# A gated-convolution and recurrence layer on one core: 1/rms by way of DRAM, one more gate group ahead, other buffers for three low halves, an earlier load of p

## The chip, the cores and the metric

One core of a Trainium2 chip runs the whole kernel in one launch. Its engines are TensorE (PE; matmuls, with the loads of weights, PEld, beside them), VectorE (DVE), ScalarE (ACT), GpSimd (POOL) and SyncE (SP). Here SP issues most loads of weights and POOL issues the other transfers. The metric is the device time of one execution in microseconds, as the median of several runs.

## What is computed

The layer takes 2,048 tokens of a prompt and 64 of a second sequence, 1,024 channels each. Cut to what matters here:

```python
h = rms_norm(x, g_pre)                       # x / rms(x) * g_pre
proj = einsum('btd,dn->btn', h, w_in)        # ten times 1,024 columns
vA, bA, cA, zA, q, f, iv, zB, gA, gB = split_cols(proj)
yA = einsum('btc,cd->btd', silu(zA) * bA * causal_conv3(cA * vA, conv_w), w_a_out)
o  = hgrn2_scan(S0, silu(q), 1 - fg, iv, log(fg))   # fg from f; 8 heads
yB = einsum('btc,cd->btd', rms(o) * g_onorm * silu(zB), w_b_out)
merged = sigmoid(gA) * yA + sigmoid(gB) * yB
x = x + rms_norm(einsum('btd,de->bte', merged, w_o), g_post)
gate = sigmoid(einsum('btd,de->bte', rms_norm(x, g_ple), w_ple_gate))
x = x + einsum('btp,pd->btd', p, w_ple_proj) * gate
```

The results are x of all tokens, the last two rows of the convolution's input and the states of the recurrence. All is float32.

## The kernel before

**Tiles and number form.** The 2,112 tokens are worked on in three blocks of 768, 704 and 640 (`SIZES`). Activations lie with the channels on the partitions: one tile is 128 channels by the tokens of a block, and eight tiles make 1,024 channels. A float32 product is made from two parts of each operand, a high one (rounded) and a low one (the rest), as three matmuls: high by high, high by low, low by high. `split` makes the parts: ScalarE casts the high one (L220, L267) and VectorE subtracts for the low one (L220).

**The seven products.** Most weights are taken in groups of two blocks of 128 columns (`sgroup`, L403). A group is a 2 x 2 scheme with seven products in place of eight. In their order (`PRODUCTS`) these use A11, S3, S1, S2, A12, A22 and S4, where S1 to S4 are sums and differences of A11, A21, A22 and A12. With 4 blocks of channels and 3 matmuls, a product is 12 matmuls and a group 84. L418, L419 and L420 are the three matmuls. Some groups make their sums from raw weights (`combined` with `first`, L335 to L356; the sums at L346); these are block 0's and two of block 1's, the first one and GB6 (the gate group of columns 6 and 7). In these two the low halves of A11, A12 and A22 already lie in DRAM and are loaded. Sums and low halves are stored to DRAM (`keep_sum`, L325; L274) for later blocks, which load them back (`kept_w`).

**The buffers of weights.** The pool `wp` has rotating buffers by tag: `raw` 5, `hi` 4, `lo` 4 and `s` 3. `sum_tile` takes an `s`; `low_tile` (L235) gives a `lo` or, in three of every seven calls, an `s`. A buffer is given again when the last reader of the old tile is done. Activations come from a ring of 48 buffers (`rt`). Matmuls write to five banks of one PSUM pool and three of another.

**The order of a block.** For each block: `path_b` (recurrence heads, with the rest of the gate groups between them), `path_a` (convolution), then the merge with W_A and W_B, the product with W_O, the two norms, and the final gate with W_G. In block 0 the merge is `merge`, with plain matmuls (L600 to L602). In blocks 1 and 2 it is `merge_in_turn`; there and in W_O the seven products of four groups take turns (`in_turn`, L533, matmuls L565 to L567, evictions L588, L590 and L459). The gates of the next block begin before the end of the present one: `run(fills, LEAD)` at L1529 runs seven of its eight gate groups, so that TensorE has work while the norms of W_O's result (`final_norm`, L1267) are made. Their steps are hung between products with `spread_out`, by a list that says how many steps each hook takes.

**1/rms of the next block.** While `path_a` runs, `row_rstd` (L713 to L732) loads x with the tokens on the partitions (L723), squares it with a sum (L729) and gets 1/rms as columns: 128 tokens each, six per block, three for each half. After the merge, `next_ops` (L1492) calls `spread_all` (L671), which for each half makes a matmul per column with the identity (`spread`, L663, matmul L668) to have the values on all partitions, and copies them from PSUM (L675). `operands` then loads x by channels (`load_x`, L710), scales it (`scaled_x`, L752) and splits it. `next_ops` is called in block 0 at step j == 6 of W_B, in block 1 at product 6 of W_B.

**p.** `load_p` (L1129) loads two tiles of p; for the last block it is called at product 5 of W_B, from POOL's queue. The other transfers of this stage there are reloads of gates and outputs (`reload`, L1175).

What sets the order on each engine is a scheduler that goes by priorities: `tc.high_priority`, `issue_after`, and dependencies. All buffers are given in the order of the program's text.

Of the kernel before, what the change touches and what calls it, by code (L numbers as in the profile page):

```python
# [18 lines left out]
P = 128  # L19
# [22 lines left out]

SWAP = 2

LEAD = 7


def plan():
# [45 lines left out]
def hybrid_step(  # L94
# [140 lines left out]
    def low_tile():  # L235

        turn[0] += 1
        if turn[0] % 7 in (1, 3, 5):
            return sum_tile(F32R)
        return wp.tile([P, 4, P], F32R, tag="lo", name=nm("lo"))  # L240
# [13 lines left out]
            return part == 1 and (idx - W_A) % KB >= KH  # L254
        return True

    def split_w(raw, key=None, spread=False):


        hi = wp.tile([P, 4, P], F32R, tag="hi", name=nm("hi"))  # L260
        if spread:
            lo = low_tile()
            split(raw, hi, lo)
            return hi, lo
        if key in lows:
            lo = low_tile()
            A.copy(hi, raw)  # L267
            SP.dma_start(lo.bitcast(F32), lows[key])
            return hi, lo
        lo = wp.tile([P, 4, P], F32R, tag="lo", name=nm("lo"))  # L270
        split(raw, hi, lo)
        if key is not None and used_later(*key):
            lows[key] = dram.tile([P, 4, P], F32, tag=f"lo{key}", name=nm("low"), bufs=1)
            stores[0].dma_start(lows[key], lo.bitcast(F32))  # L274
        return hi, lo
# [59 lines left out]
    def combined(i1, i2, first, anew):  # L335


        with tc.high_priority():
            if not first:
                return {n: kept_w(i1, i2, n, spread=anew) for _, n, _, _, _ in PRODUCTS}  # L340
            a11, a21, a22, a12 = (load_raw(w_blk[i, h]) for i, h in ((i1, 0), (i2, 0), (i2, 1), (i1, 1)))
            out = dict(A11=split_w(a11, (i1, 0)))

            def total(name, x, y, op):
                s = sum_tile()
                V.tensor_tensor(s, x, y, op)  # L346
                out[name] = keep_sum(name, i1, s)
                return s

            total("S3", a11, a21, ALU.subtract)  # L350
            s1 = total("S1", a21, a22, ALU.add)
            s2 = total("S2", s1, a11, ALU.subtract)
            out["A12"] = split_w(a12, (i1, 1))
            out["A22"] = split_w(a22, (i2, 1))
            total("S4", a12, s2, ALU.subtract)
            return out  # L356

# [310 lines left out]
                T.matmul(pb[:, o : o + P], cols[:, i : i + 1].to_broadcast([P, P]), ident, start=True, stop=True)  # L668
        return pb[:, :n]

    def spread_all(cols):  # L671

        rs = rt()
        for h in range(2):
            A.copy(half(rs, h), spread(cols[h], hn()))  # L675
        return rs

    def col_rstd(acc, n):

        pc = ps_attn()  # L680
# [31 lines left out]

    def row_rstd(bl, out):  # L713

        out.extend(cols_tile(hn()) for _ in bl["segs"])
        todo = [(cols, s["t0"] + o, i) for cols, s in zip(out, bl["segs"]) for i, o in tiles_of(hn())]
        nxt = []
        for n in range(0, len(todo) + 2, 2):
            now, nxt = nxt, []
            for cols, o, i in todo[n : n + 2]:  # L720
                xts = [rt(512), rt(512)]
                for q, xt in enumerate(xts):
                    G.dma_start(xt, x_tok[o : o + P, q * 512 : q * 512 + 512])  # L723
                nxt.append((cols, i, xts))
            for cols, i, xts in now:
                sc = small.tile([P, 2], F32, tag="ss2", name=nm("ss2"), bufs=2)
                with behind_all(copies):
                    for q, xt in enumerate(xts):
                        A.activation(xt, xt, AF.Square, accum_out=sc[:, q : q + 1])  # L729
                V.tensor_tensor(sc[:, 0:1], sc[:, 0:1], sc[:, 1:2], ALU.add)  # L730
                rstd_of(sc[:, 0:1], cols[:, i : i + 1], 1.0 / D)
            yield  # L732

    def sums_of(hc, pair):

# [88 lines left out]
    def gates(bl, hc, kept, first):  # L824


        groups = [(kind, j) for kind in (GA, GB) for j in range(0, KB, 2)]
        for kind, j in groups[: -1 if first else None]:
            outs = [rt(), rt()]
            n = groups.index((kind, j))  # L830
            sgroup(kind * 8 + j, kind * 8 + j + 1, hc, gate_sink(outs), first, by_k=n == 0 and not first, anew=n < LEAD)
            keep_gates(kept, kind, j, outs)
            yield

# [626 lines left out]
    for bi, bl in enumerate(blocks):  # L1461
# [30 lines left out]
        def next_ops():  # L1492

            with sized_to(nxt):
                made = sized(nxt, operands(hc, spread_all(cols), partial(load_x, nxt)))
                next(made)
            return made

        if nxt:
# [24 lines left out]
        if nxt:  # L1524
            xo.extend(stages[-1]["mid"])
            fills = sized(nxt, gates(nxt, hc, kepts[bi + 1], False))
            norm = sized(bl, final_norm(bl, segs, xo, acc, h2, kept))
            spread_out((norm, (1, 1, 1, 1, 0, 1, 0, 1) + (0, 1) * KB + (0, 0, 0, 0, 1, 0, 1) + (0, 1) * KB))
            run(fills, LEAD)  # L1529
            assert not hooks  # L1530
            run(final_gate(bl, segs, xo, h2, kept))
        else:
            gate = [final_gate(bl, [s], xo, h2, kept, anew=s is segs[1]) for s in segs]
            spread_out((norms[0], (2, 2, 1, 0, 1, 1, 4, 4)), (norms[1], (0,) * 6 + (1, 1) + (1, 2, 2, 2, 1, 1, 1, 3, 3, 2)))
            run(ple(bl, ph, kept, spare=range(KB)))
            run(gate[0])
            assert not hooks
            run(gate[1])
# [49 lines left out]
```

## Time and profile before

| | us |
|---|---|
| median of 3 runs | 2606.26 |
| the three runs | 2603.63, 2606.26, 2608.92 |
| profiled execution | 2604.98 |
| its span in the profile | 2603.2 |
| granted TensorE clock over the span | 0.999 of full speed |

The stages of the profiled execution by TensorE's work, in us from the start of the span:

| stage | from | to |
|---|---|---|
| p's products and a first gate group | 0 | 77.5 |
| block 0: groups of seven products | 77.5 | 700.6 |
| block 0: W_A and W_B (plain) | 700 | 841 |
| block 0: W_O in turn | 841 | 901 |
| seven gate groups of block 1 | 901 | 1003 |
| block 0: final gate, W_G | 1003 | 1070 |
| block 1: the other groups, heads | 1070 | 1585 |
| block 1: W_A, W_B, W_O in turn | 1585 | 1750 |
| seven gate groups of block 2 | 1750 | 1845 |
| block 1: final gate | 1845 | 1907 |
| block 2: the other groups, heads | 1907 | 2368 |
| block 2: W_A, W_B, W_O in turn | 2368 | 2522 |
| block 2: p's products, final gate, outputs | 2522 | 2603 |

How to read the lines of the profile: a group is named by its line in the kernel, its engine, its operation and `out<-in`. A time in brackets behind an instruction is the idle time of its engine before it, and the arrow names what ended it. In the windows, each pair is the busy time of an engine and the number of its instructions; then come the granted TensorE clock (1.00 is full), the busy share of the DMA engines and the GB/s that they moved.

### The profile page before, as it was taken

Reading aid. Unit: us, or ns where it says so; the run is one execution under the profiler, and the core shown is the slowest. Engines: PE = TensorE matmul, PEld = TensorE weight load, DVE = VectorE, ACT = ScalarE, POOL = GpSimd, SP = SyncE. Lnnn points to the kernel's source line nnn. Section 1 sums busy time; section 2 is a strip of 40 time slices with the busy share of each in tenths; the row PEclk is TensorE's granted clock in tenths of the full one; section 3 lists DMA queues with packets and bytes.
Section 4 is the critical chain, followed back from the end, with each engine's and each line's share of the span. In section 5 each row is a group of like instructions: output and inputs, shape, how many; then the busy total and the mean of one; then the engine's idle time right before and its main releaser. Section 6 shows DMA issues by size and latency. Waiting matters only on the chain.

```text
span 2603.2 us, 47398 instructions
## 1 busy us (share of the span) xinstructions
PE 2579.6 (99%) x16484; PEld 2566.8 (99%) x16484; DVE 1729.1 (66%) x3469; ACT 1487.7 (57%) x2896; POOL 358.5 (14%) x665
## 2 busy tenths in 40 slices
PE   8999999999999999999999999999999999999999
PEld 8999999999999999999999999999999999999998
DVE  7887788788777775465564556887435555336867
ACT  6655565554443664466565555567456665446675
POOL 2000000110154021111111221102100000001111
PEclk9999999999999999999999999999999999999999
DMA  8677667798799898866778999989887878999986
GB/s 324 220 240 247 233 221 242 269 304 264 264 359 353 274 328 270 284 221 205 259 226 277 357 390 313 321 287 322 302 271 243 274 245 264 299 298 318 333 271 202
DMA packets 355681, 728.42 MB, mean 280 GB/s; under 512 B 43601, under 2 KB 48241, under 8 KB 355441
## 3 DMA queue, kind: packets, MB, share of 16 engines
q1 hardware_dynamic: 316656, 573.52, 66.2%
q0 software_dynamic: 38496, 151.83, 16.0%
q8 instruction: 130, 2.13, 0.3%
q14 instruction: 111, 0.90, 0.1%
q10 hardware_dynamic: 288, 0.05, 0.0%
HBM read 532.00 MB, written 193.22 MB: 279 GB/s over the span
## 4 chain that ended last, share of the span: by engine, by line
PE 92%; DMA 4%; DVE 1%; issue 1%; ACT 1%; POOL 0%; SPq 0%; DVEq 0%; POOLq 0%; ACTq 0%
PE pg L418 20%; PE pg L420 19%; PE pg L419 19%; PE pg L565 4%; PE pg L566 4%; PE pg L567 4%; PE pg L600 3%; PE pg L602 3%; PE pg L601 3%; PE pa L1045 1%; PE pa L1081 1%; PE pa L1083 1%; DMA lo<-low 1%; PE pa L1031 1%; PE pa L1030 1%
## 5 line engine op out<-in xcount | busy, mean ns | idle before, releaser
L418 PE MATMUL pg<-r,hi 128*128 128x320 f32 (+2 forms) x3304 | 1085.6, 329 | 0.3 <-ACT r L809 0.3
L419 PE MATMUL pg<-r,hi 128*128 128x320 f32 (+2 forms) x3304 | 1068.3, 323 | 0.0
L420 PE MATMUL pg<-r,lo 128*128 128x384 f32 (+2 forms) x2356 | 768.3, 326 | 3.8 <-DMA lo<-low 3.8
L267 ACT CAST hi<-raw 128x512 fp32r<-128x512 f32 x706 | 435.0, 620 | 501.4 <-PE pg L419 169.5
L418 PEld LDWEIGHTS pg<-r,hi 128*128 128x128 f32 x3304 | 621.8, 188 | 1.0 <-ACT r L809 0.6
L419 PEld LDWEIGHTS pg<-r,hi 128*128 128x128 f32 x3304 | 622.1, 188 | 0.0
L420 PEld LDWEIGHTS pg<-r,lo 128*128 128x128 f32 x2356 | 442.8, 188 | 4.9 <-DMA lo<-low 4.9
L420 PE MATMUL pg<-r,s 128*128 128x352 f32 (+1 forms) x948 | 299.8, 316 | 1.5 <-DMA s<-low 1.5
L220 ACT CAST hi<-raw 128x512 fp32r<-128x512 f32 x260 | 158.8, 621 | 160.4 <-PE pg L419 47.8
L566 PE MATMUL pg<-r,hi 128*128 128x320 f32 (+2 forms) x752 | 239.1, 320 | 0.0
L565 PE MATMUL pg<-r,hi 128*128 128x320 f32 (+2 forms) x752 | 237.1, 320 | 0.0
L600 PE MATMUL pg<-r,hi 128*128 128x384 f32 (+2 forms) x640 | 211.0, 331 | 2.6 <-ACT hi L220 2.4
L601 PE MATMUL pg<-r,hi 128*128 128x384 f32 (+2 forms) x640 | 210.8, 330 | 0.0
L220 DVE TENSOR_TENSOR lo<-raw,hi 128x512 fp32r<-128x512 f32 x232 | 158.2, 686 | 72.9 <-ACT hi L220 70.7
L220 DVE TENSOR_TENSOR r<-r,r 128x320 fp32r<-128x320 f32 (+7 forms) x298 | 177.5, 616 | 42.4 <-ACT r L220 40.8
L220 ACT CAST hi<-s 128x512 fp32r<-128x512 f32 x160 | 99.2, 620 | 173.8 <-PE pg L419 161.6
L602 PE MATMUL pg<-r,lo 128*128 128x384 f32 (+2 forms) x560 | 185.6, 332 | 0.2 <-DVE lo L220 0.2
L420 PEld LDWEIGHTS pg<-r,s 128*128 128x128 f32 x948 | 178.3, 188 | 2.3 <-DMA s<-low 2.3
L220 ACT CAST r<-r 128x320 fp32r<-128x320 f32 (+7 forms) x298 | 157.7, 562 | 23.1 <-DVE r L741 4.2
L432 ACT COPY hf<-pg 128x352 f32<-128x352 f32 (+2 forms) x354 | 156.2, 444 | 2.1 <-PE pg L420 1.9
L567 PE MATMUL pg<-r,lo 128*128 128x320 f32 (+2 forms) x484 | 153.8, 319 | 2.1 <-DMA lo<-low 2.1
L220 DVE TENSOR_TENSOR lo<-s,hi 128x512 fp32r<-128x512 f32 x160 | 110.1, 689 | 65.8 <-ACT hi L220 63.0
(393 smaller groups left out, 4186.2 us busy)
## 6 DMA issues: line engine op xcount, KB each, us to landing
raw<-w_blk SPq DMA_DIRECT2D x582, 256.0 KB, 4.1
raw<-S SPq DMA_DIRECT2D x424, 256.0 KB, 4.1
lo<-low SPq DMA_DIRECT2D x414, 256.0 KB, 4.1
s<-low SPq DMA_DIRECT2D x292, 256.0 KB, 4.1
low<-lo SPq DMA_DIRECT2D x275, 256.0 KB, 3.3
S<-s SPq DMA_DIRECT2D x152, 256.0 KB, 3.0
r<-w_blk POOLq DMA_DIRECT2D x48, 256.0 KB, 6.7
S<-r POOLq DMA_DIRECT2D x48, 256.0 KB, 6.4
```

The lines of the kernel that those rows point to most:

```text
L220: return A.copy(hi, src).ins, V.tensor_tensor(lo, src, hi.bitcast(F32), ALU.subtract).ins
L267: A.copy(hi, raw)
L418: add(hi[:, k, :], xhi, start=start and k == 0, stop=False)
L419: add(hi[:, k, :], xlo, start=False, stop=False)
L420: last[0] = add(lo[:, k, :], xhi, start=False, stop=k == KH - 1).ins
L432: copied = A.copy(got[n], ps[bank])
L565: add(hi[:, k, :], xhi, start=start and k == 0, stop=False)
L566: add(hi[:, k, :], xlo, start=False, stop=False)
L567: last[0] = add(lo[:, k, :], xhi, start=False, stop=k == KH - 1).ins
L600: T.matmul(ps, hi[:, k % 4, :], xhi[:, c], start=k == ks[0], stop=False)
L601: T.matmul(ps, hi[:, k % 4, :], xlo[:, c], start=False, stop=False)
L602: last[0] = T.matmul(ps, lo[:, k % 4, :], xhi[:, c], start=False, stop=k == ks[-1]).ins
```

## The change

It has four parts. First, `row_rstd` goes over the whole block (six columns for 704 tokens, five for 640), writes the columns to a row in DRAM, and `broadcast` spreads the row over all partitions with one DMA; `spread_all` is gone. `ask_rs` issues that DMA at step j == 4 of W_B in block 0 and at product 4 of W_B in block 1; `next_ops` stays where it was. Second, `LEAD` is (7, 8): at the end of block 1 all eight gate groups of block 2 run ahead of the final gate, with a new list of steps for the norms; the eighth goes by the loaded low halves (`anew` is true for the first seven only). Third, in `combined` the loaded low halves of A11, A12 and A22 always take `lo` buffers and no longer an `s` in some of the calls. Fourth, the last block's p is asked for at the start of W_A.

```diff
-LEAD = 7
+LEAD = (7, 8)
...
-    def split_w(raw, key=None, spread=False):
+    def split_w(raw, key=None, spread=False, among_sums=False):
...
         if key in lows:
-            lo = low_tile()
+            lo = wp.tile([P, 4, P], F32R, tag="lo", name=nm("lo")) if among_sums else low_tile()
...
-            out = dict(A11=split_w(a11, (i1, 0)))
+            out = dict(A11=split_w(a11, (i1, 0), among_sums=True))
...
-            out["A12"] = split_w(a12, (i1, 1))
-            out["A22"] = split_w(a22, (i2, 1))
+            out["A12"] = split_w(a12, (i1, 1), among_sums=True)
+            out["A22"] = split_w(a22, (i2, 1), among_sums=True)
...
-    def spread_all(cols):
-
-        rs = rt()
-        for h in range(2):
-            A.copy(half(rs, h), spread(cols[h], hn()))
-        return rs
...
-        out.extend(cols_tile(hn()) for _ in bl["segs"])
-        todo = [(cols, s["t0"] + o, i) for cols, s in zip(out, bl["segs"]) for i, o in tiles_of(hn())]
+        todo = tiles_of(bl["n"])
+        full = bl["n"] // P
+        cols = small.tile([P, 2, 6], F32, tag="rows", name=nm("rows"), bufs=1)[:, 0, : len(todo)]
...
+            if n >= len(todo):
+                row = dram.tile([BN], F32, tag="xrs", name=nm("xrs"), bufs=2)[: bl["n"]]
+                G.dma_start(row[: full * P].rearrange("(i p) -> p i", p=P), cols[:, :full])
+                if full < len(todo):
+                    G.dma_start(row[full * P :].rearrange("(p o) -> p o", o=1), cols[(full + 1) * P - bl["n"] :, full : full + 1])
+                out.append(row)
             yield
+
+    def broadcast(row):
+
+        t = rt()
+        G.dma_start(t, row.partition_broadcast(P))
+        return t
...
-            sgroup(kind * 8 + j, kind * 8 + j + 1, hc, gate_sink(outs), first, by_k=n == 0 and not first, anew=n < LEAD)
+            sgroup(kind * 8 + j, kind * 8 + j + 1, hc, gate_sink(outs), first, by_k=n == 0 and not first, anew=n < LEAD[0])
...
-                made = sized(nxt, operands(hc, spread_all(cols), partial(load_x, nxt)))
+                made = sized(nxt, operands(hc, x_rs[0], partial(load_x, nxt)))
                 next(made)
             return made
+
+        def ask_rs():
+            with sized_to(nxt):
+                x_rs.append(broadcast(cols[0]))
...
+                if j == KB - 4:
+                    ask_rs()
                 if j == KB - 2:
...
+        if bl["last"]:
+            ps = load_p(bl, G)
         for idx, n in in_turn(stages, a_first):
             loads(idx, n)
-            if nxt and (idx, n) == (W_B, 6):
+            if nxt and (idx, n) == (W_B, 4):
+                ask_rs()
+            elif nxt and (idx, n) == (W_B, 6):
                 spread_out((next_ops(), (0, 1, 0, 1, 0, 1, 0) * KH))
             elif nxt:
                 pass
             elif (idx, n) == (W_B, 5):
-                ph = [split_rt(raw) for raw in load_p(bl, G)]
+                ph = [split_rt(raw) for raw in ps]
...
-            spread_out((norm, (1, 1, 1, 1, 0, 1, 0, 1) + (0, 1) * KB + (0, 0, 0, 0, 1, 0, 1) + (0, 1) * KB))
-            run(fills, LEAD)
+            if first:
+                steps = (0, 1) * KB + (0, 0, 0, 0, 1, 0, 1) + (0, 1) * KB
+            else:
+                steps = (0, 1, 0, 1, 0) * KH + (0, 0, 0, 0, 1, 0, 0, 1) + (0, 1, 0, 1, 0) * KH
+            spread_out((norm, (1, 1, 1, 1, 0, 1, 0, 1) + steps))
+            run(fills, LEAD[bi])
```

More of the change, by code (lines that the diff above doesn't have):

```diff
@@ L719, in row_rstd @@
             now, nxt = nxt, []
-            for cols, o, i in todo[n : n + 2]:
+            for i, o in todo[n : n + 2]:
                 xts = [rt(512), rt(512)]
                 for q, xt in enumerate(xts):
-                    G.dma_start(xt, x_tok[o : o + P, q * 512 : q * 512 + 512])
-                nxt.append((cols, i, xts))
-            for cols, i, xts in now:
+                    G.dma_start(xt, x_tok[bl["t0"] + o : bl["t0"] + o + P, q * 512 : q * 512 + 512])
+                nxt.append((i, xts))
+            for i, xts in now:
                 sc = small.tile([P, 2], F32, tag="ss2", name=nm("ss2"), bufs=2)
@@ L1494, in next_ops @@
             with sized_to(nxt):
-                made = sized(nxt, operands(hc, spread_all(cols), partial(load_x, nxt)))
+                made = sized(nxt, operands(hc, x_rs[0], partial(load_x, nxt)))
                 next(made)
             return made
+        def ask_rs():
+            with sized_to(nxt):
+                x_rs.append(broadcast(cols[0]))
+        x_rs = []
         if nxt:
```

## The prediction

> **What bounds the kernel now.** I read the page first: the busy times and the shares of the chain that ended last.
>
> ```profile
> span 2603.2 us, 47398 instructions
> PE 2579.6 (99%) x16484; PEld 2566.8 (99%) x16484; DVE 1729.1 (66%) x3469; ACT 1487.7 (57%) x2896; POOL 358.5 (14%) x665
> PE 92%; DMA 4%; DVE 1%; issue 1%; ACT 1%; POOL 0%; SPq 0%; DVEq 0%; POOLq 0%; ACTq 0%
> ```
>
> TensorE is busy 2579.6 of 2603.2 us, and 92% of the chain is TensorE. So only two things can shorten the kernel: fewer matmuls, or shorter waits of TensorE. All that it does not work is 23.6 us. Next comes the view of TensorE's waits over the whole run (engine, line, releaser: us in total, times, longest).
>
> ```profile
> PE pa L1152 <- ACT r L220: 6.9, 1, 6.9
> PE pg L420 <- DMA lo<-low: 3.8, 4, 1.8
> PE pg L600 <- ACT hi L220: 2.4, 1, 2.4
> PE pg L567 <- DMA lo<-low: 2.1, 2, 1.3
> PE pg L420 <- DMA s<-low: 1.5, 2, 1.0
> ```
>
> The first is the start of the kernel and the third the turn of block 0; the change touches neither. The rest, 3.8 + 2.1 + 1.5 = 7.4 us, are waits for low halves of weights that come back from DRAM. Third, the windows around those places, with the granted clock and the DMA share as third and second figure from the end.
>
> ```profile
> core 0: us, PE busy (x) PEld busy (x) DVE busy (x) ACT busy (x) POOL busy (x), PEclk, DMA share, GB/s
> 1070.00:1084.00 14.00, 14.00 (x88) 14.00 (x87) 6.45 (x10) 7.18 (x14) 2.48 (x5) 1.00 0.97 366
> 1240.00:1250.00 10.00, 10.00 (x65) 10.00 (x64) 7.01 (x17) 5.32 (x12) 2.69 (x5) 1.00 0.91 310
> 1253.00:1259.00 6.00, 5.57 (x31) 5.50 (x32) 0.00 (x0) 2.15 (x5) 0.54 (x1) 0.72 1.03 386
> 1784.00:1798.00 14.00, 12.55 (x82) 11.77 (x82) 9.48 (x15) 6.24 (x12) 2.04 (x4) 1.00 1.02 395
> 2360.00:2380.00 20.00, 20.00 (x136) 19.73 (x136) 19.94 (x44) 13.39 (x30) 0.55 (x2) 1.00 0.81 256
> 2440.00:2451.00 11.00, 9.67 (x65) 9.26 (x64) 7.04 (x18) 9.30 (x24) 0.26 (x1) 1.00 0.96 349
> ```
>
> The waits stand where the DMA share is about 1. One of them also cost clock: 0.72 over 6 us is 0.28 x 6 = 1.7 us of matmul time.
>
> **Part 1, 1/rms by way of DRAM.** Removed: two spreads of 12 matmuls each, with four ScalarE copies behind them.
>
> ```profile
> 831.56 1.34 PE pa L668 x12
> 1693.39 1.34 PE pa L668 x12
> L668 PE MATMUL pa<-ident,cols x96: 271/275/377, 831.4 to 2561.9; 128*128 128x128 f32 x96
> ```
>
> Both stand on the chain of waits with 1.34 us, so -2 x 1.34 = **-2.7 us**. It is matmul time with no cover, so both bounds are 2.7.
>
> Added: the columns of 1/rms go to a DRAM row, and one DMA spreads the row over 128 partitions. They hang on POOL's queue.
>
> ```profile
> 578.23 1.40 POOL L657 TENSOR_TENSOR cols<-cols,mhalf 128x1 f32<-128x1 f32 x2 [7.69 <-DVE cols L655]
> 1474.21 0.76 POOL L657 TENSOR_TENSOR cols<-cols,mhalf 128x1 f32<-128x1 f32 x1 [1.18 <-DVE cols L655]
> 810.79 0.54 POOL L1175 DMA_DIRECT2D r<-g__169_763  x1
> 1656.57 0.54 POOL L1175 DMA_DIRECT2D r<-g__3594_15065  x1
> 1667.07 0.54 POOL L710 DMA_DIRECT2D r<-x_fm  x1 [9.96 <-DVE r L220]
> r<-x_fm POOLq DMA_DIRECT2D x16, 352.0 KB, 6.8
> ```
>
> The last columns are ready at 578 and 1474, and the broadcasts are issued beside the reloads at about 811 and 1657. So the stores, element by element, have over 180 us to land; their cover is that whole stretch, and without it their latency would stand before the broadcast. The Trainium skill, "DMA: Bandwidth & Descriptors", section "Rules for kernel authors", says that a last dimension that isn't contiguous becomes one descriptor per element, which speaks against such a store; no run shown here has its price, and by either reading the sum stays as it is.
>
> The trace has no broadcast. The nearest row has the same size, 128 rows of 352 KB in all: 6.8 us. So it lands at about 1657 + 7 = 1664, before the first x tile, which is asked for at 1667. Its reader is L752 on VectorE. In block 1 the change moves the first two L752 from behind the spread to just behind the second L1219.
>
> ```profile
> 1675.29 0.53 DVE L1219 TENSOR_TENSOR r<-hf,r 128x352 f32<-128x352 f32 x1
> 1677.97 0.52 DVE L459 TENSOR_TENSOR hf<-r,pg 128x352 f32<-128x352 f32 x1
> 1684.53 0.32 PE L565 MATMUL pg<-r,hi 128*128 128x352 f32 x1
> 1697.26 0.87 DVE L752 SCALAR_TENSOR_TENSOR r<-r,vec,r 128x640 f32<-128x640 f32 x1
> ```
>
> Behind a waiting L752 stand the additions L459 that empty the matmuls' banks, and behind them TensorE. With five banks, the third L459 (1677.97) frees the one that the matmul at 1684.53 fills: 1684.53 - 1677.97 - 0.52 = 6.0 us of slack, so x or the row may come at about 1682. The x tile: 1667.07 + 0.54 + 6.8 is 1674.4, just before L752's turn. The two L752 themselves take 2 x 0.87 = 1.7 us of the 6.0. So **0**; above it, nothing until a landing passes 1682 - 1.7 = 1680. In block 0 the move is shorter (L752 passes the last L1207 only, and two x loads go ahead of eight of POOL's), and I price it the same. One x_tok tile fewer (two loads, two squares) is off the path: VectorE and ScalarE are busy 66% and 57%.
>
> **Part 2, the low halves off the sums' buffers.** It acts in two groups of block 1: the first (1070 to 1084) and one that starts at about 1240.
>
> ```profile
> 1236.43 0.68 DVE L346 TENSOR_TENSOR s<-raw,raw 128x512 f32<-128x512 f32 x1
> 1238.44 0.68 DVE L346 TENSOR_TENSOR s<-s,raw 128x512 f32<-128x512 f32 x1
> 1241.11 5.51 DMA low<-lo
> 1246.67 6.72 DMA lo<-low
> 1253.43 0.43 PE L420 MATMUL pg<-r,lo 128*128 128x352 f32 x1 [1.83 <-DMA lo<-low]
> lo<-low SPq DMA_DIRECT2D x414, 256.0 KB, 4.1
> ```
>
> The chain reads: A12's low half sits in one of three buffers of the sums, so S1 and S2 come late; S1's low half is stored (5.51), the store frees a buffer, only then the next group's low half is fetched (6.72), and TensorE waits 1.83 us and then runs at half clock. With the three buffers free for the sums, that fetch goes, by the order of the two programs, to one freed about two matmul products earlier. A product is 12 matmuls at 10/65 us, 1.85 us, so 3.7 us earlier beats 1.83. Gone: 1.83 + 1.7 = **-3.5 us**; bounds 0 and -3.5. I take the whole, because the store that leads the chain is the thing removed.
>
> A rule speaks against half of this. The Trainium skill, "TensorE: Matmul & The Clock Gate", section "Part 1: The HAM clock gate", has the clock fall only after an idle window of about 3.4 us; the row shows 0.72 around a wait of 1.83, and 1.00 around the waits of 1784 to 1798. By the rule the lost clock isn't this wait's, and the sum would be 1.7 us smaller; I follow the row.
>
> The price: A12's and A22's low halves now wait for the same group's products 0 and 1 to free their buffers, and are needed three products later, 3 x 1.85 = 5.5 us, against a median landing of 4.1 and the 6.72 above. Bounds: 0, and 4 x (7.0 - 5.5) = 6.0 us without clock (7.02 is shown in part 4). I take **+0.3**, near the median.
>
> **Part 3, eight groups ahead.** TensorE's work is the same; the eighth group moves from about 2040 to before the last gate, and its 14 loads with it. The waits that can ease are those of 1784 to 1798, where loads, spills of x and stores fill the queues:
>
> ```profile
> PE pg L420 <- DMA lo<-low: 1.1, 2, 0.8
> PE pg L420 <- DMA s<-low: 1.0, 1, 1.0
> PE pg L418 <- ACT r L809: 0.3, 1, 0.3
> ```
>
> These are 2.4 us from 1740 to 1800; 14.00 - 12.55 = 1.45 of TensorE's idle time lies in the window of 1784. In the order of the two programs the spills and fetches stretch over 171 matmuls in place of 161: 6% more room, where the DMA share is 1.02. So little: **-0.6**, bounds -1.5 and +0.5 (new loads in a full stretch).
>
> **Part 4, p asked for ahead.**
>
> ```profile
> 2439.19 1.08 POOL L1129 DMA_DIRECT2D r<-p_fm  x2 [4.58 <-DVE r L576]
> 2441.97 7.02 DMA lo<-low
> 2449.03 0.41 PE L567 MATMUL pg<-r,lo 128*128 128x320 f32 x1 [1.33 <-DMA lo<-low]
> ```
>
> Two loads of 320 KB start 2.8 us before a low half that takes 7.02 in place of 4.1, and TensorE waits 1.33. In the change they go out at about 2361, behind four reloads, where the share is 0.81. **-1.0**; bounds -1.3, and +0.7 if the same collision happens there for one wait of half that size.
>
> **Sum.** -2.7 - 3.5 + 0.3 - 0.6 - 1.0 = -7.5 us. The profiled execution took 2604.98 us (span 2603.2 and 1.8 around it), which gives 2597.5. The median of the runs shown, 2606.26, is 1.28 above that execution: **2598.8 us**.
>
> **Rivals.**
> - *The sums' group still waits* (15%): only part 2 fails, because the next fetch takes another late buffer. For it: DMA share 1.03 there. Against: the chain names the store. 2598.8 + 3.5 = 2602.3.
> - *The DMA-bound places keep their waits* (10%): parts 3 and 4 save nothing. For it: shares of 1.02 and 0.96 move waits rather than end them. 2598.8 + 1.6 = 2600.4.
> - *Low halves of A12 and A22 arrive late* (10%), the slower side: each of the four loads lands in 7.0 us against 5.5, and each group pays the clock once: 4 x 1.5 + 2 x 1.7 = 9.4 in place of 0.3, so 2598.8 + 9.1 = 2607.9. It decides from a landing of 6.9 us on (1.36 each gives 8.8, less 0.3 and the 7.5 of the sum). For it: shares of 0.97 and 0.91 in both groups and the 6.72 of the neighbour. Against: the median of 4.1.
> - *The clock isn't this wait's* (5%): a later drop falls elsewhere, 2598.8 + 1.7 = 2600.5; this is the result that the rule of the clock gate above would give.
> - *Other waits go too* (6%): the idle time of the window of 1784 goes whole, 0.85 more, and the other 0.95 of the 2.4 us of 1740 to 1800 with it: 2598.8 - 1.8 = 2597.0.
> - *The change doesn't take effect on the path* (4%): the broadcast lands late, behind POOL's reloads. From 1680 on each microsecond costs one; the gain of 7.5 is gone at about 1688, 31 us after the issue, four to five times the 6.8 of the row. 2606.3.
>
> **How the numbers follow.** That leaves 50% for the forecast. About 0.2% (5.2 us) is what a measurement of this kernel can tell from no change, so faster means below 2601.05 and slower above 2611.5. The runs shown lie 2.7 us to either side of their median. Faster: forecast 0.80, other waits 0.9, DMA-bound and clock 0.6 each, the sums' group 0.3, slower side and no effect 0.05: 0.40 + 0.05 + 0.09 + 0.045 + 0.01 = 0.60. Slower needs the late low halves at their worst and one more wait: 0.07. The rest, 0.33, is the same. Range: the lower end takes parts 3 and 4 at their best (-1.2 more) with the clock and run scatter (about -5.5): 2592; the upper takes the late low halves at about 2607 and leaves their worst out: 2592 to 2607.
>
> **What would show it.** L668 has 24 matmuls fewer. Part 1 is right if the first L752 of block 1 ends its wait before 1680 (as times of before), and TensorE has no wait for L459 or L1219 there. Part 2 is right if no wait stands at the head after the sums' group and its clock is 1.00; wrong if L420 waits for lo<-low within three products of either group. Part 3: the waits of the stretch ahead of the last block, 2.4 us. Part 4: p issued before the first product of W_A, no L567 wait of 1.3. A wait of TensorE of over 2 us at a new place would make the forecast wrong.

## The result and the profile after

| | us |
|---|---|
| before, median of 8 runs | 2605.83 (2601.98 to 2611.07) |
| changed, median of 8 runs | 2613.18 (2610.89 to 2621.08) |
| ratio changed / before | 1.0028, 95% interval 1.0018 to 1.0038 |
| profiled execution of the change | 2616.87 (its span 2615.2) |

The change is slower by 0.28%, some 7.3 us, where 7.5 us less were forecast. In the page of the changed kernel TensorE is busy for almost the same time (2581.2 us for 2579.6, with 24 matmuls fewer), and the span is 12 us longer; so most of the time lies in waits, and some in the half clock that follows a few of them.

```profile
span 2615.2 us, 47352 instructions
PE 2581.2 (99%) x16460; PEld 2565.2 (98%) x16460; DVE 1728.2 (66%) x3467; ACT 1486.8 (57%) x2888; POOL 361.7 (14%) x667
PE 90%; DMA 6%; issue 1%; DVE 1%; ACT 1%; POOL 1%; SPq 0%; DVEq 0%; POOLq 0%; ACTq 0%
```

TensorE's waits by releaser in the changed kernel (us in total, times, longest):

```profile
PE pg L420 <- DMA lo<-low: 8.5, 8, 2.6
...
PE pg L600 <- ACT hi L220: 3.3, 2, 2.7
PE pg L567 <- DMA lo<-low: 3.1, 1, 3.1
PE pg L420 <- DVE lo L220: 1.4, 2, 0.8
PE pg L567 <- DMA s<-low: 1.0, 1, 1.0
```

L420 waited 3.8 us for low halves before; it is 8.5 now. The chain of waits in order of time names the loads and stores that it waited for, each with its start and its time to landing; five of the longest, in excerpt:

```profile
582.09 14.66 DMA low<-lo
...
841.39 8.38 DMA lo<-low
...
1487.00 13.18 DMA lo<-low
1500.25 11.59 DMA lo<-low
...
1796.63 10.27 DMA lo<-low
```

Three of the five stand just behind a place where the change added something: at 579 and at 1479 POOL stores a row element by element. The windows there, of the changed kernel:

```profile
579.00:592.00 13.00, 13.00 (x76) 13.00 (x75) 8.54 (x13) 6.69 (x13) 3.52 (x4) 1.00 1.11 134
1479.00:1491.00 12.00, 12.00 (x76) 12.00 (x75) 4.03 (x6) 6.84 (x14) 4.46 (x9) 1.00 1.07 203
1491.00:1513.00 22.00, 17.84 (x105) 16.39 (x104) 11.01 (x21) 7.53 (x15) 5.69 (x12) 1.00 1.00 383
```

And of the kernel before, at the same matmuls as the first two (the changed kernel is 6.6 us behind it at the second):

```profile
579.00:592.00 13.00, 13.00 (x76) 13.00 (x75) 11.31 (x19) 6.63 (x13) 0.93 (x2) 1.00 0.79 262
1472.30:1484.30 12.00, 12.00 (x76) 12.00 (x75) 5.82 (x12) 8.82 (x21) 4.85 (x10) 1.00 1.03 370
```

The last two figures of a row tell it: with the store the DMA engines are at least as busy (1.11 for 0.79, 1.07 for 1.03) and move little more than half as much (134 for 262 GB/s, 203 for 370). The low halves that SP stores beside the first one (L274) land after 11.6 to 14.7 us, for 2.0 to 4.5 before. TensorE still works through the 12 us of the store on what was loaded; then it has 17.84 of 22 us.

### The profile page after: what moved, and what is told of

Read it like the earlier page. It is cut to its first block, busy times and chain, and to the rows that moved or that the text cites. A ratio compares the mean times of both kernels' runs of the same rounds, so it can differ in the third digit from the quotient of the medians.

```text
span 2615.2 us, 47352 instructions
## 1 busy us (share of the span) xinstructions
PE 2581.2 (99%) x16460; PEld 2565.2 (98%) x16460; DVE 1728.2 (66%) x3467; ACT 1486.8 (57%) x2888; POOL 361.7 (14%) x667
## 4 chain that ended last, share of the span: by engine, by line
PE 90%; DMA 6%; issue 1%; DVE 1%; ACT 1%; POOL 1%; SPq 0%; DVEq 0%; POOLq 0%; ACTq 0%
PE pg L418 19%; PE pg L420 19%; PE pg L419 19%; PE pg L565 4%; PE pg L566 4%; PE pg L567 4%; DMA lo<-low 3%; PE pg L600 2%; PE pg L601 2%; PE pg L602 2%; PE pa L1087 1%; PE pa L1051 1%; PE pa L1089 1%; DMA low<-s 1%; PE pa L1037 1%
## 5 line engine op out<-in xcount | busy, mean ns | idle before, releaser
L420 PE MATMUL pg<-r,lo 128*128 128x384 f32 (+2 forms) x2368 | 772.8, 326 | 10.0 <-DMA lo<-low 8.5
L420 PEld LDWEIGHTS pg<-r,lo 128*128 128x128 f32 x2368 | 444.7, 188 | 13.6 <-DMA lo<-low 11.0
L420 PE MATMUL pg<-r,s 128*128 128x320 f32 (+1 forms) x936 | 296.3, 317 | 0.5 <-DMA s<-low 0.5
L566 PE MATMUL pg<-r,hi 128*128 128x320 f32 (+2 forms) x752 | 240.6, 321 | 0.4 <-DVE r L220 0.4
L420 PEld LDWEIGHTS pg<-r,s 128*128 128x128 f32 x936 | 176.3, 188 | 1.5 <-DMA s<-low 1.5
L567 PE MATMUL pg<-r,lo 128*128 128x320 f32 (+2 forms) x472 | 150.9, 320 | 3.1 <-DMA lo<-low 3.1
```

What stands on the lines that cost most here:

```text
L420: last[0] = add(lo[:, k, :], xhi, start=False, stop=k == KH - 1).ins
L566: add(hi[:, k, :], xlo, start=False, stop=False)
L567: last[0] = add(lo[:, k, :], xhi, start=False, stop=k == KH - 1).ins
```

## The experiments

Eighteen kernels ran. Beside each ratio stands its 95% interval. A profile shows one execution, and all the profiles cover the same matmuls. So this table takes seven stretches of the profile before (us from its start) and the matmuls at their two ends, and gives for every kernel's profile how much longer (or shorter, in us) it took from the one to the other. It is worked out from the start times of the matmuls, without those of the spreads and of the dense row.

```
                 576-682  734-898 1149-1295 1438-1583 1680-1730 1730-2360 2360-2496
before               0.0      0.0       0.0       0.0       0.0       0.0       0.0
p_only               0.0      3.4      -1.8       0.2       0.0      -1.7       2.0
before_dummy         0.0     -0.6      -2.4       0.0       0.0      -1.7       0.0
shift_only           0.0      6.2      -3.8       0.0       0.0       3.3      -1.5
sums_only            0.0      2.9      -2.4       0.0       0.0       1.2      -1.5
sums_again           0.0      3.7       1.0       0.0       0.0       3.8      -1.8
sums_turn            0.0      7.1       3.6       0.0       0.0      -1.4       0.9
no_p1                0.0     -0.2      -1.6       0.5       0.0       3.0      -1.5
p1_only              0.2      5.1      -1.0       4.3      -1.0      -1.2       0.4
the change           2.3      6.8      -2.3       5.5      -1.2       2.4      -1.9
late_both            0.0      3.9      -1.6       3.7      -1.0       2.5      -1.7
row_twice            4.4      2.7      -2.6       5.3      -0.9       1.6      -1.7
row_dense            0.5     -0.6      -2.5       0.4      -0.6       0.5      -1.5
dense_lead7          0.5      5.3      -1.7       0.4      -0.5       2.7       1.2
dense_oldsteps       0.5      4.6      -1.7       0.4      -0.9       3.1      -1.7
dense_late_both      0.5      4.6      -1.7       0.2      -0.8       4.3      -1.9
dense_old0           0.0      5.7      -1.8       0.5      -1.0       3.0      -1.8
dense_p              0.5      4.4      -2.0       0.4      -1.3       0.6      -1.6
gb6_dense            0.5      2.8      -1.7       0.4       1.0      -1.1      -1.1
gb6_dense_p          0.5      2.7      -2.3       0.4      -1.3      -2.4      -0.4
```

**Which part is it?** Part 1 alone (the kernel before with the row and its broadcast), and the change without part 1:

> The kernel before with part 1 alone (1/rms by way of DRAM). Theory A (the element-wise stores of the row hold the DMA engines for some 10 us each, so that weights and low halves come late, and in block 0 the broadcast and the earlier loads of x delay the stores that the turn of W_O waits for): in the profile of the change these places cost 2.3 at 594 to 628, 5.2 between 792 and 853 and 5.5 at 1494 to 1512, and the second removed spread gives 1.2, so before + 11.8, range +8 to +13; the wait of 1.83 at 1253 stays. Rival B (part 1 is harmless and the loss is the eighth gate group's and the buffers'): before - 2.7, the two spreads.

> The change without part 1: the old spread, with the buffers, the eight groups and p as changed. Theory A: what is left is -1.3 (buffers), +2.5 (the stretch ahead of the last block) and -1.9 (p), so before - 0.7, range -4 to +2. Rival B: after + 2.7 or more, that is before + 10.

Measured: p1_only 1.0024 (1.0015 to 1.0033), no_p1 1.0019 (1.0009 to 1.0029). Both halves lose. Rival B falls with the first. A is not right in size either: the 6 us of p1_only (3.9 to 8.6 by its interval) are under most of the 8 to 13 that it had, and no_p1's 5 us (2.3 to 7.6) are outside its -4 to +2, so parts 2 to 4 have a loss of their own.

**The store.** row_dense makes rows of the columns before they are stored. Its store also goes out one step of `side` later, at 617 and 1500 us in place of 579 and 1479:

```diff
+        with placed():
+            T.matmul(pt[: len(todo), :P], cols, ident, start=True, stop=True)
+        A.copy(flat[: len(todo)], pt[: len(todo), :P])
-                G.dma_start(row[: full * P].rearrange("(i p) -> p i", p=P), cols[:, :full])
+        G.dma_start(row[: full * P].rearrange("(i p) -> i p", p=P), flat[:full])
...
-                if 1 <= j <= 4:
+                if 1 <= j <= 5:
```

> The change, but the columns are first turned into rows by one small matmul with the identity and a ScalarE copy, so that the row goes to DRAM as five or six pieces of 512 bytes in place of 704 or 640 of 4 bytes. Theory A: the loads around the store land in 3 to 7 us again in place of 11 to 15, no waits at 594 and 1494 to 1512, after - 7.8 (2.3 and 5.5), range -5 to -9. Rival C (the stores take long but what TensorE waits for there is late for another reason, such as the order of the queues): after, within 2 us.

row_twice makes the large store a second time:

```diff
+                G.dma_start(again[: full * P].rearrange("(i p) -> p i", p=P), cols[:, :full])
```

> The change with the element-wise store of 640 elements made twice (the second into a row that nothing reads). Theory A: another 9 to 10 us of held DMA engines at each of the two places, with nothing left to hide them: after + 10 to + 20. Rival C, or a store whose latency alone counts: after, within 2 us.

row_dense: 1.0000 (0.9992 to 1.0009), 7.3 us under the change's ratio. Its windows at the matmuls of the rows above (579, 1468.4 and 1480.4) and at its own store (617 and 1500):

```profile
579.00:592.00 13.00, 13.00 (x76) 13.00 (x75) 11.31 (x18) 6.74 (x13) 1.03 (x2) 1.00 0.82 266
617.00:629.00 12.00, 12.00 (x70) 12.00 (x69) 9.44 (x17) 4.48 (x8) 1.07 (x2) 1.00 0.84 270
1468.40:1480.40 12.00, 12.00 (x77) 12.00 (x76) 8.52 (x14) 7.74 (x16) 7.11 (x14) 1.00 1.02 362
1480.40:1497.00 16.60, 16.60 (x105) 16.60 (x104) 6.92 (x14) 7.76 (x15) 1.12 (x4) 1.00 1.04 401
1500.00:1512.00 12.00, 12.00 (x76) 12.00 (x75) 7.62 (x14) 7.24 (x15) 5.71 (x13) 1.00 0.98 347
```

The rates are back (266 and 362 GB/s), and the 105 matmuls that took 22 us take 16.6. Where the dense store itself runs there is no dip (270 and 347) and no wait of TensorE; it lands in 4.4 to 4.5 us. In the table's fourth column the four kernels with the element-wise store have 3.7 to 5.5, all others 0.5 at most: the store is the cause there, and rival C falls. Shape and place of the store changed together; what an element-wise store would cost at the later place was not run.

How much the dense row wins is less sure than that. Four other kernels with the dense row and part 2 (dense_lead7, dense_oldsteps, dense_late_both and dense_old0, below) are 2.1 to 4.7 us slower than the kernel before, so only 2.6 to 5.2 under the change.

row_twice came out at 1.0045 (1.0033 to 1.0058), some 4 us above the change and not 10 to 20. In block 1 its second store cost nothing (5.3 for 5.5): the two landed 10.6 and 9.9 us after their issues, 0.9 us apart, so the price isn't simply one per element. In block 0 the profile has 4.4, half clock included; the three kernels with one store have 0.0 to 2.3 there, so how much of it is the second store's is not shown.

**Block 0's merge (734 to 898).** The change's profile lost 6.8 us here, and four kernels asked whether the broadcast or the earlier loads of x cause it. late_both asks for both later; dense_late_both has the dense row beside that; dense_old0 has the old spread in block 0; before_dummy adds the broadcast's load alone:

```diff
-                if j == KB - 4:
-                    ask_rs()
                 if j == KB - 2:
                     a_first.extend(narrow(half(t, 0)) for t in mg[:KH])
-                    ops = next_ops()
+                    ask_rs()
+            ops = next_ops()
```

```diff
+                if j == KB - 4:
+                    G.dma_start(spare, x_fm[:P, :704])
```

> The change, but in block 0 the broadcast is asked for two steps later (at j == 6 of W_B) and x's first two loads one step later, so that POOL's queue has them behind most of the stores of sums and low halves, as in the kernel before; the element-wise stores of the row stay. Theory D (the broadcast and the x loads push back the chain of stores from which the turn of W_O gets its low halves): the waits at 833 to 850 go (0.6 + 0.8 + 1.0 + 3.1 and 6.8 us at half clock), after - 5, range -3 to -7. Rival E (what is late there is an echo of the element-wise store at 579): after, within 1.5 us.

> The dense row together with the later broadcast and x loads of block 0. The profile of row_dense has no wait at 825 to 855, so there is little to win in that execution; in its other runs (5.8 us longer in the median) there may be. Theory D: row_dense - 2, range 0 to -4. Rival E: row_dense, within 1 us.

> The dense row, but only for block 1's end: in block 0 the old spread with its matmuls is back, so no row, no broadcast and x's loads where they were; parts 2 to 4 as changed. Theory H (in block 0's full stretch the broadcast's 352 KB and the x loads ahead of it are what makes the turn's low halves late, beside the stores): no waits of over 1 us at 825 to 855, and the median at row_dense - 1 to + 1, since it gives up 1.3 us of removed matmuls and wins some 3 us of waits that the dense kernels' profiles show there in three of four. Rival I (these waits come from parts 2 to 4 or from the runs' scatter): waits of 3 us at 842 to 850 again, row_dense + 1.3.

> The kernel before with one more DMA from POOL's queue at j == 4 of block 0's W_B: 352 KB of x from DRAM to DRAM, read by nobody. It is the load of the broadcast without its buffer, its reader or any other order. Theory H: waits at 842 to 850 of 1 to 3 us appear, before + 1 to + 5. Rival I or an order effect: before, within 0.7 us in the profile's stretch from 789 to 855.

Measured: late_both 1.0028 (1.0017 to 1.0040), dense_late_both 1.0016 (1.0007 to 1.0025), dense_old0 1.0018 (1.0008 to 1.0029), before_dummy 0.9995 (0.9986 to 1.0004). Theories D and H fall, and E with them: the loss stands in dense_old0 (5.7), whose block 0 is the one before. It stands even in p_only, which changes nothing ahead of 2360. A wait of TensorE in p_only:

```profile
845.23 0.68 PE L567 MATMUL pg<-r,lo 128*128 128x384 f32 x1 [2.97 <-DMA lo<-low]
```

So this is scatter of the kernel itself. Of the nine profiles whose block 0 has no part 1 (before_dummy among them), three are without the loss (before, before_dummy, no_p1) and six have 2.9 to 7.1; their mean is 3.1, and that of the eleven with part 1 in block 0 is 3.8. What is left for part 1 here is 0.7 us, less than the scatter of these means (about 1.1 us, an estimate from the two sets). In this stretch the profile from which the prediction was made was one of the lucky ones.

**Ahead of the last block (1730 to 2360).** The change's profile waits here longer than before, and its chain names a load of 10.27 us. Was it the eighth group, its list of steps, or something else?

> The dense row with seven groups ahead and the old list of steps (parts 1, 2 and 4 of the change). If the eighth group costs what the profiles of the change and of the kernel without part 1 show ahead of the last block (2.5 and 2.4 us): row_dense - 2, range -0.5 to -3.5. By the prediction's sum (part 3 saves 0.6): row_dense + 0.6.

> The dense row with eight groups ahead, but with the old list of steps for the norms, so that the transfers of x keep their old places. Theory F (the list is what makes x's transfers and the weights' loads collide at 1784 to 1808): like dense_lead7, row_dense - 2. Rival G (the list changes nothing; a wait stands where the DMA engines are full, whatever the group): row_dense, within 1 us.

> The kernel before with part 2 alone, as changed. From the profiles of the change: the stall at 1253 goes, with 0.8 at 1087, 0.4 at 1251 and 0.5 at 1258 in its place, -1.3 to -2.5. Theory J (the six calls of low_tile that part 2 no longer makes shift the alternation between lo and s buffers, and the wait of 2.6 to 2.9 us ahead of the last block at 1797, with its half clock, comes from that): + 2.5 there, before + 0.5, range -1 to +2. Rival K (that wait belongs to the eighth group or the stretch's scatter): 1797 as in the kernel before, before - 2, range -0.5 to -3.5.

> Part 2 alone, with the counter of the alternation kept going, so that every later low half gets the kind of buffer it had before. Theory J: no wait over 1 us at 1784 to 1808 and full clock there, sums_only - 2.5, before - 2. Rival K: like sums_only.

```diff
         if key in lows:
+            turn[0] += among_sums
             lo = wp.tile([P, 4, P], F32R, tag="lo", name=nm("lo")) if among_sums else low_tile()
```

dense_lead7: 1.0013 (1.0004 to 1.0022), dense_oldsteps: 1.0008 (1.0000 to 1.0017); neither is faster than row_dense, and the wait stands with seven groups as with eight. sums_only: 1.0024 (1.0011 to 1.0036). Part 2 alone is slower, though its profile, which happened to be the shortest of its runs, is not. With the counter kept (sums_turn, 1.0036, 1.0024 to 1.0049) the wait here is gone, but the kernel is slower still, where J expected 2 us less than before. A wait of 4.71 us stands inside the sums' group GB6, at the first use of A12's low half:

```profile
1257.11 0.66 PE L421 MATMUL pg<-r,lo 128*128 128x352 f32 x1 [4.71 <-DMA lo<-low]
```

Two more kernels part the counter from the buffers. shift_only has nothing of part 2 but its side effect: the counter by which `low_tile` alternates is set back after each of the two groups, as if it hadn't been called.

```diff
+            kept_turn = turn[0]
             a11, a21, a22, a12 = (load_raw(w_blk[i, h]) for i, h in ((i1, 0), (i2, 0), (i2, 1), (i1, 1)))
...
             total("S4", a12, s2, ALU.subtract)
+            turn[0] = kept_turn
             return out
```

> The kernel before, with only the counter of the alternation set back after the groups that make sums from raw weights and have their low halves in DRAM, so that later low halves get the kinds of buffers that they have in the change. Theory J (the shifted alternation is what brings the wait of 2 to 3 us ahead of the last block): waits of 2 to 3 us at 1790 to 1808, with a half clock in some, before + 2.3, range 0 to + 4. Rival K: no such wait, before within 1 us.

> Part 2 alone once more, for a second profile. If the first profile (2604.60, the shortest of its runs) missed a loss at the sums' groups, this one shows at 1250 to 1260 a wait of over 2 us with half clock, as sums_turn's did (4.7 and 6.8 us at half clock). If the loss is the shifted alternation's, it shows 2 to 3 us at 1796 again and under 1 us at 1250 to 1260. Time as in sums_only, 2608.8 within 3.

shift_only's profile has the wait, and so has sums_again's:

```profile
1799.11 0.42 PE L422 MATMUL pg<-r,lo 128*128 128x320 f32 x1 [2.82 <-DMA lo<-low]
```

```profile
1802.50 0.64 PE L420 MATMUL pg<-r,lo 128*128 128x320 f32 x1 [2.82 <-DMA lo<-low]
```

In the table's sixth column the twelve kernels with the shifted counter have 0.5 to 4.3, mean 2.6; the eight with the old one have -2.4 to 0.6, mean -1.1. The shift costs 3.7 us. Of the twelve, the eight with eight groups have 2.5 on average and the four with seven 2.7: the eighth group changes nothing that these profiles can tell. One matmul shows it best: the same one in all the profiles (at 1794.32 in the profile before, 1795.81 in sums_only) waits 1.87 to 3.05 us for its low half in all twelve kernels with the shifted counter, and 0.60 at most in the eight others. So J stands for this wait, and F and K fall; of G it holds that neither the list nor the group changes anything. What the shift does is seen on SP's queue, first in sums_only:

```profile
1783.00 0.42 SPq L268 DMA_DIRECT2D s<-low  x1
1784.27 0.33 SPq L230 DMA_DIRECT2D raw<-w_blk  x1
1784.65 1.49 SPq L268 DMA_DIRECT2D lo<-low  x2
```

and at the same stretch in the kernel before:

```profile
1782.11 0.46 SPq L268 DMA_DIRECT2D lo<-low  x1
1783.42 0.32 SPq L230 DMA_DIRECT2D raw<-S  x1
1783.87 0.40 SPq L268 DMA_DIRECT2D lo<-low  x1
```

In both these loads take 10.6 to 12.5 us to land; the DMA share is 1.02 from 1784 to 1798 in the kernel before. There, that matmul's low half is asked for at 1782.11 and takes 12.2 us, and TensorE waits 0.31. In sums_only it is asked for at 1784.65, while TensorE wants it at 1792.9, 8 us later. That its buffer comes free later with the other alternation is inferred from the program's text; the wait for the buffer itself was not followed. TensorE then waits:

```profile
1795.81 0.41 PE L420 MATMUL pg<-r,lo 128*128 128x320 f32 x1 [2.90 <-DMA lo<-low]
```

But the times don't make the counter the cause of part 2's loss. shift_only is 1.0005 (0.9993 to 1.0017), 1.3 us and no loss that can be told: its sums' group gains what the last block loses (-3.8 and 3.3 in the table). sums_again is 1.0023 (1.0014 to 1.0031): part 2 with the shift costs 6 us, twice measured, and part 2 without it 9.4 (6.3 to 12.8). So what loses time over the whole kernel is part 2's own step, the three low halves that may only take `lo` buffers, and in these profiles the shift moves a part of it from the sums' groups to the stretch ahead of the last block. Two waits inside these groups show it: in sums_again one of 2.33 us for A22's low half (0.49 in sums_only), half clock behind it, and sums_turn's 4.71 for A12's.

```profile
1255.03 0.43 PE L420 MATMUL pg<-r,lo 128*128 128x352 f32 x1 [2.33 <-DMA lo<-low]
```

sums_again's load was asked for at 1247.98 and took 7.00 us. In sums_turn's chain a store of a sum (3.57 us) and two issues on SP's queue go ahead of A12's load (6.52 us).

**A version that beats both?** dense_p has parts 1 (dense) and 4 alone, p_only part 4. gb6_dense has the dense row, and the shift for GB6 alone with the old alternation from there on; gb6_dense_p has part 4 too.

```diff
+            if turn[0] != kept_turn:
+                turn[0] = kept_turn + (6 if i1 == GB * 8 + KB - 2 else 0)
```

> Parts 1 (with the dense row) and 4 alone: no change of the buffers, seven groups ahead. From the profiles' terms: -2.4 (two spreads, less one small matmul) and -1.7 (p): before - 4, range -1 to -6. If part 1 costs in block 0's full stretch whatever the store, before + 0 to + 2.

> Part 4 alone. The profiles show -1.6 to -1.9 at 2375 to 2450 in every kernel that has it: before - 1.7, range 0 to -3; by the prediction's sum -1.0.

> Part 1 with the dense row; part 2 replaced by setting the alternation back by three between block 1's first group and GB6 and forward again after it, so that GB6's low halves sit as in shift_only (whose profile has no stall at 1250 to 1260) and everything later as in the kernel before; seven groups ahead, p as before. The stall of 1.8 us and its half clock go (-3.5), no wait over 1.5 us at 1784 to 1808, and the spreads give -2.4 less 0.5 for the dense store's matmul: before - 5, range -2 to -7. If the gain at 1253 comes back as a wait elsewhere: before - 2 or less.

> The same with part 4. If the earlier p gives what the profiles of the change showed at 2437 to 2451 (-1.6): gb6_dense - 1.6, before - 6.5, range -3 to -8. If its new waits at 2375 to 2391 (1.9 us in p_only) take that back: gb6_dense within 1 us.

Measured: dense_p 0.9996 (0.9988 to 1.0005), p_only 1.0004 (0.9995 to 1.0013), gb6_dense 0.9996 (0.9985 to 1.0007), gb6_dense_p 0.9995 (0.9984 to 1.0005). All beat the change; none beats the kernel before by more than can be told. The expected 4 to 6.5 us are not there: the terms had been read against one profile before, in which the stall at 1253 was followed by half clock (third column: four other kernels without part 2 or the shift have -1.0 to -2.4 there) and the merge was at its best. Nor did the shift for GB6 alone take the stall away: the two kernels wait 1.90 and 1.34 us at that matmul.

## Why the prediction was wrong, step by step

**Part 1, the removed matmuls: right, smaller.** L668 has 24 fewer (source view of the changed kernel, against x96):

```profile
L668 PE MATMUL pa<-ident,cols x72: 270/275/377, 932.7 to 2573.5; 128*128 128x128 f32 x72
```

The second spread's place (1680 to 1730) is 0.5 to 1.3 shorter in all but one of the kernels that lack it, against the 1.34 of the chain.

**Part 1, the row's stores: this step failed.** It said that the stores "have over 180 us to land; their cover is that whole stretch". That is true of their own landing, in 11.4 to 12.0 us:

```profile
DMA to landing us min/median/max: 11.4/11.7/12.0
```

But it only asked who waits for the store. Nobody does; yet while it runs, all the others move little more than half as much. Loads and stores issued beside it land up to 14.66 us after their issue (the chain's rows above), and TensorE pays: 0.8 us in block 0 (mean of the change, p1_only and late_both; 0.0 to 2.3) and 4.5 in block 1 (3.7 to 5.5). The Trainium skill, "DMA: Bandwidth & Descriptors", section "Issuing engines are not separate DMA queues", says that transfers from all engines run on the same 16 DMA engines and interleave there. The traces agree: POOL's store slows SP's loads. Together with the sentence on one descriptor per element that the prediction cites, this points to a loss; the prediction had that sentence and let it touch only the latency.

**Part 1, broadcast and L752: right.** No bank waited for it: TensorE has no wait at all from 1670 to 1745 in the changed kernel. In block 1 the first scaling ran at 1688.01 (1675.8 in the time of before, where 1680 was the limit), with no idle time before it:

```profile
1688.01 0.88 DVE L758 SCALAR_TENSOR_TENSOR r<-r,vec,r 128x640 f32<-128x640 f32 x1
```

**Part 2: this step failed too.** It was to win 3.5 us for a price of 0.3; alone it costs 6 us. What it removes was read rightly: the wait of 1.83 us is gone in every kernel with part 2, and the seven kernels that have neither part 2 nor the full shift wait 1.12 to 2.04 at that matmul. But its half clock, half of the 3.5, is in one of these seven profiles alone. And the price was mis-sized. In the eleven kernels with part 2 and the shift TensorE waits in GB6 at the first matmul with S1 (0.38 to 0.49 us) and, in ten of them, for A22's low half (0.40 to 2.33, mean 1.05); in sums_turn for A12's (4.71). In the changed kernel it waits for A12's in the first group and for A22's in GB6:

```profile
1087.15 0.43 PE L420 MATMUL pg<-r,lo 128*128 128x352 f32 x1 [0.81 <-DMA lo<-low]
1257.94 0.43 PE L420 MATMUL pg<-r,lo 128*128 128x352 f32 x1 [0.54 <-DMA lo<-low]
```

That is the rival "low halves of A12 and A22 arrive late", with one late load in a group and not four, and it is the prediction's own sign that part 2 is wrong. So from 1149 to 1295 the eleven have -1.7 on average, and the five with neither part 2 nor the shift have -1.4: a gain of 0.3 us in place of 3.2.

The working also missed that `low_tile` is a counter: six calls fewer change the kind of buffer of every later low half, which costs 3.7 us ahead of the last block. That is not a loss by itself, as shift_only's time shows; without the shift, part 2 loses more at the sums' group (3.6 in the table). By these profiles part 2 with its shift costs 3.4 us, by the times of sums_only and sums_again about 6 (2.9 to 9.4 and 3.6 to 8.1). Where the rest lies is open: their two profiles, of the same program, are 8 us apart.

**Part 3: near.** -0.6 was forecast, with bounds of -1.5 and +0.5; by the means above it is -0.2.

**Part 4: the mechanism right, the size not.** p went out where it was said, behind four reloads:

```profile
2374.02 1.07 POOL L1135 DMA_DIRECT2D r<-p_fm  x2
```

That is 2360.5 in the time of before. From 2360 to 2496 the twelve profiles with it have -1.0 on average and the eight without -0.6, so some -0.5 in place of -1.0; p_only's time shows nothing. The L567 wait is gone in the changed kernel, and TensorE waits 0.4 us for a split at L566; in p_only these waits are 2.1 us.

**The sum again, from means.** Stores 0.8 + 4.5, block 0's merge 0.7 (its removed spread within it), the second spread -0.8, part 2 -0.3 + 3.7, part 3 -0.2, part 4 -0.5: together +7.9, against the 7.3 measured (4.7 to 9.9). That they come so near is in part luck, since most terms are means of single executions. The sign of the whole hangs on two steps, the stores and part 2; without these two it would be -0.8.

## What to carry to other kernels

Ask of each added transfer not only who waits for it, but what it holds while it runs: where the DMA share is high, 640 elements of 4 bytes cost as much as some 2 MB of rows (the 128 to 167 GB/s missing over 12 to 13 us), and making them rows first cost TensorE about half a microsecond. Buffers taken from one use are bought from another: ask which tile will now wait for which reader, in the same group, before counting the wait that goes. A counter or ring that hands out buffers is part of the schedule: whoever takes a few calls out of it moves every later choice, so follow it to the end of the kernel. And where one term is a single stall of one profile, look at whether it is the same in a second profile before it is counted in full.

## What the runs showed of the hardware

**The clock falls by half of a window.** In each profile the half-clock stretches lie on one grid of 3.413 us. In the twenty profiles (up to 2590 us) 39 windows of that grid run at half clock behind one at full clock. In 38 of them TensorE had been idle for 1.70 us or more of the window ahead, in one for 0.74. Between 1.70 and 1.83 us it goes either way (five windows were followed by half clock, six not), above 1.83 always, and below 1.70 only in that one. So half a window is the limit, and the same wait costs clock or not by where it falls: p_only's 2.97 us at 845 lies in one window, and its clock is 0.83 over ten microseconds, while the 2.90 us of sums_only at 1795.81 lie across two (1.1 and 1.8, the second where it goes either way) and its clock stays full.

```profile
842.00:852.00 10.00, 7.03 (x32) 6.77 (x31) 4.95 (x10) 4.21 (x10) 0.00 (x0) 0.83 0.89 319
```

The Trainium skill, "TensorE: Matmul & The Clock Gate", section "Part 1: The HAM clock gate", has the window right, 3413 ns and running free, but asks for a whole idle window; here half of one is enough, and the measurement decides.

**A store of 4-byte elements.** 640 elements from 128 partitions took 11.4 to 12.0 us in the changed kernel (9.4 to 11.7 in p1_only and late_both), and the core moved 134 and 203 GB/s meanwhile, for 262 and 370 at the same matmuls without it. Stored as five rows of 512 bytes they landed in 4.4 to 4.5 us in row_dense.
